# Two of the weights' four quarter sums made by accumulating DMAs, the other two written in place over them

## The chip, the cores and the metric

The kernel runs on one core of a Trainium2 chip. The metric is the device time of one execution in microseconds (us), and the median of three is compared. One core has a matrix engine (PE), a vector engine (DVE), a scalar engine (ACT), a general engine (POOL) and a sequencer that issues transfers (SP); each works through its own queue in order, and semaphores tie the queues together. Sixteen DMA engines move data between the memory and the on-chip buffers.

## The reference, cut to what matters

The reference is a decoder trunk of two layers over 528 tokens (16 learned ones and 512 given) of width 1024, all in float32:

```python
h = concat(meta_tokens, x)
for i in range(2):
    h = h + 0.5 * swiglu(rmsnorm(h, norm_ffn1[i]), ffn1_w_in[i], ffn1_w_out[i])   # 1024 -> 2 x 2816 -> 1024
    hn = rmsnorm(h, norm_mix[i])
    h = h + (retention(hn) if i == 0 else gla(hn))
    h = h + 0.5 * swiglu(rmsnorm(h, norm_ffn2[i]), ffn2_w_in[i], ffn2_w_out[i])
return rmsnorm(h, final_norm)[:, 16:]
```

`swiglu` is `(silu(x @ gate) * (x @ up)) @ out`. Retention and GLA are chunked linear attentions between projections of the same width. All that matters for the change is that nearly all the work is products of activations with large weights, each of which is read from memory once, and that every product is to be as exact as float32.

## The kernel before, in words

**Products.** The tokens lie along the free axis in two halves of 264 (256 in the last stage). A weight tile of 128x128 is the stationary operand of a matmul, the activations the moving one. For exactness each operand is held as two parts of a shorter format, `hi` and `lo`, and each product is three matmuls (`mm3`, lines 311 to 313): hi by hi, hi by lo, lo by hi.

**Units.** Most large products are done as a *unit* (`unit`, line 473 and on): two neighbouring weight tiles, cut in two halves each, make a 2x2 block of quarters a11, a12, a21, a22, the two token halves make the other side, and seven products replace eight (a Strassen-Winograd scheme). The seven use the pieces `a11, s1, s2, a12, s3, s4, a22`, where four are sums of the weights' quarters:

```python
SUMS = {"s1": ("a21", "a22"), "s2": ("s1", "a11"), "s3": ("a11", "a21"), "s4": ("a12", "s2")}
```

A piece is 128x512 (four 128x128 tiles), or 128x384 where the group of hidden tiles is six wide instead of eight. A unit has thus 7 x 4 x 3 = 84 matmuls, or 63 with narrow pieces. The program has 134 units, 24 of them narrow. The two SwiGLUs of each layer start with a phase of eight plain products (lines `p`, tiles `pf...`), during which the sums of the activations are prepared; then come units for gate (`Xf10g`, `QZf10g`), up (`...u`) and output (`...o`). Retention has some plain products and units, GLA plain products only.

**Weights.** The class `Weights` (line 54 and on) holds a plan of all pieces in the order of use. `_load` starts transfers of whole tiles of 128x1024 on SP's queue into four places (`raw`, 512 KB each, line 91); a unit needs two of them. `_piece` finds a quarter in a `raw` tile, or makes a sum with an addition on DVE into a `ws` tile (line 107). `_split` (lines 121 and 122) makes the two parts of a piece: `whi` is a copy with rounding on ACT, `wlo` the difference on DVE. There are seven places for `whi` and seven for `wlo`. After each product a call of `hook` asks for the split of the next four pieces, so the code runs at least that far ahead of the products; a place is free again when the last matmul on it has ended.

**Order.** Each engine's queue order is laid down when the program is built, by a scheduler that goes by the dependences, the program order and its own costs; code under `urgent()` is drawn forward by 300 steps. At run time every engine takes its queue strictly in order.

**Around the sums.** Besides the weights, DVE also adds up a unit's results (lines 664 to 676 for the output units), and in the last output group of a SwiGLU it prepares the next stage: for every finished row block of `x` it makes the `ula` part of the scaled activations (line 384) and a running sum of squares (line 392). Then come the statistics of the norm: matmuls `st_n` on PE, `ms_n` on DVE (line 427), a power on POOL (`rc`, line 429), `dg_n` on DVE (line 431), and `bc_n` on PE (line 438), which spreads the row factors. POOL has nothing else to do before the change.

Of the kernel before, what the change touches and what calls it, by code (L numbers as in the profile page):

```python
# [16 lines left out]
P = 128  # L17
# [37 lines left out]
class Weights:  # L55

    UNIT = ("a11", "s1", "s2", "a12", "s3", "s4", "a22")
    FIRST = ("s1", "s2", "a11", "a12", "s3", "s4", "a22")  # L60
    SUMS = {"s1": ("a21", "a22"), "s2": ("s1", "a11"), "s3": ("a11", "a21"), "s4": ("a12", "s2")}

    def __init__(self, tc, ctx, raw_bufs=4, bufs=7):
        self.nc = tc.nc
        self.raw_pool = ctx.enter_context(tc.tile_pool(name="wraw", bufs=raw_bufs))
        self.pool = ctx.enter_context(tc.tile_pool(name="wsplit", bufs=bufs))
        self.raw_bufs, self.bufs = raw_bufs, bufs
        self.chunks, self.raw = [], {}
        self.plan, self.parts, self.sums = [], {}, {}
        self.loaded = self.done = self.split = self.taken = 0  # L70
        self.live = set()
        self.sum_pool = None

    def add(self, key, ap):
        n = ap.shape[1]
        c = len(self.chunks)
        self.chunks.append(ap)
        for o in range(0, n, PW):
            self.plan.append((key, c, o, min(PW, n - o), o + PW >= n))

    def add_unit(self, key, ap1, ap2, order):
        c = len(self.chunks)
        self.chunks += [ap1, ap2]
        for q in order:
            self.plan.append((key + (q,), c, q, ap1.shape[1] // 2, {"s4": c, "a22": c + 1}.get(q)))

    def _load(self):
        while self.loaded < min(self.done + self.raw_bufs, len(self.chunks)):
            ap = self.chunks[self.loaded]
            t = self.raw_pool.tile([P, CW], F32, tag="raw", name=f"raw{self.loaded}")  # L90
            self.nc.sync.dma_start(t[:, :ap.shape[1]], ap)
            self.raw[self.loaded] = t
            self.loaded += 1

    def _piece(self, c, q):

        V = self.nc.vector
        if not isinstance(q, str):
            return self.raw[c][:, q:q + PW]
        n = self.chunks[c].shape[1] // 2  # L100
        if q[0] == "a":
            o = (int(q[2]) - 1) * n
            return self.raw[c + int(q[1]) - 1][:, o:o + n]
        if (c, q) not in self.sums:
            a, b = [self._piece(c, i) for i in self.SUMS[q]]
# [1481 lines left out]
```

## Time and profile before

| | us |
|---|---|
| median of three runs | 2142.69 (2142.47 to 2145.72) |
| the profiled execution | 2141.96 |
| its span in the trace | 2140.2 |
| PE busy in it | 2103.9 |
| DVE busy in it | 1868.0 |
| ACT busy in it | 1146.0 |
| POOL busy in it | 21.8 |
| bytes read from memory | 196.42 MB |

The page counts an engine as busy between the start and the modelled end of its instructions. Matmuls overlap, so PE counts as busy whenever one is in flight, and its idle time is only what remains. A row such as `PE Xf10o L311 <- ACT whi L121: 2.7, 3, 1.2` says: matmuls of line 311 into the tile `Xf10o` waited 2.7 us in all for ACT's `whi` of line 121, three times, 1.2 us at the longest. In a row of the table by stretches the number after x is how many instructions started in the stretch. Buffer numbers are left out of names, so `raw` stands for all raw tiles.

### The profile page before, as it was taken

The page shows a single profiled execution, that of the slowest core. Times are in us where ns is not written, and L with a number is a line of the kernel's source. Part 1 is how long each engine was busy: PE and PEld are TensorE (multiplying, and loading weights), DVE is VectorE, ACT ScalarE, POOL GpSimd, SP SyncE. Part 2 cuts the span into 40 slices and gives each one's busy share as a digit, 9 for nine tenths or more (in the row PEclk, how much of TensorE's full clock was granted, in tenths as well). Part 3 has the DMA queues.
Part 4 walks back from the last instruction along what each step waited for, and adds up shares of the span by engine and source line. Part 5 has one row for each costly group of instructions (what it writes and reads, how often), then busy time and mean ns, then how long its engine had stood idle before and what let it go on. Part 6 is the DMA issues. An engine that isn't in the chain of part 4 may idle for free.

```text
span 2140.2 us, 42535 instructions
## 1 busy us (share of the span) xinstructions
PE 2103.9 (98%) x16950; PEld 2069.3 (97%) x16950; DVE 1868.0 (87%) x3451; ACT 1146.0 (54%) x2220; POOL 21.8 (1%) x25
## 2 busy tenths in 40 slices
PE   8999999999999999999999999999999999999998
PEld 7999999999999999999998999999899999999998
DVE  7999999977686879999999999989876658999996
ACT  5656656443434354656566565656733235656654
POOL 0000000000000000000000000000000000000000
PEclk9999999999999999999999999999999999999999
DMA  4333323332222222232323233332312112233332
GB/s 142 98 110 100 103 93 92 100 110 82 97 80 96 83 71 79 90 109 99 109 93 96 80 109 103 97 107 86 122 60 66 63 62 78 87 121 99 104 109 75
DMA packets 59175, 201.26 MB, mean 94 GB/s; under 512 B 6624, under 2 KB 8032, under 8 KB 58976
## 3 DMA queue, kind: packets, MB, share of 16 engines
q1 hardware_dynamic: 57968, 195.26, 28.5%
q10 hardware_dynamic: 1008, 3.29, 0.5%
q8 instruction: 133, 2.18, 0.4%
q14 instruction: 66, 0.54, 0.1%
HBM read 196.42 MB, written 2.10 MB: 93 GB/s over the span
## 4 chain that ended last, share of the span: by engine, by line
PE 79%; DVE 15%; ACT 2%; DMA 2%; issue 2%; POOL 0%; SPq 0%; DVEq 0%; POOLq 0%; ACTq 0%
DVE wlo L122 4%; DVE ws L107 2%; PE po_r L313 1%; PE po_r L311 1%; PE po_r L312 1%; PE lv L1227 1%; DVE hf L340 1%; PE Xf21o L311 1%; PE Xf20o L311 1%; DMA raw<-in_f_in 1%; PE Xf20g L311 1%; PE Xf20g L312 1%; PE Xf20g L313 1%; PE Xf20u L311 1%; PE Xf11g L311 1%
## 5 line engine op out<-in xcount | busy, mean ns | idle before, releaser
L121 ACT CAST whi<-raw 128x512 fp32r<-128x512 f32 (+1 forms) x613 | 369.1, 608 | 393.2 <-PE gv L312 51.0
L121 ACT CAST whi<-ws 128x512 fp32r<-128x512 f32 (+1 forms) x536 | 322.3, 603 | 340.9 <-DVE ws L107 86.8
L122 DVE TENSOR_TENSOR wlo<-raw,whi 128x512 fp32r<-128x512 f32 (+1 forms) x613 | 402.9, 668 | 67.6 <-ACT whi L121 65.8
L122 DVE TENSOR_TENSOR wlo<-ws,whi 128x512 fp32r<-128x512 f32 (+1 forms) x536 | 349.5, 659 | 27.6 <-ACT whi L121 25.5
L107 DVE TENSOR_TENSOR ws<-raw 128x512 f32<-128x512 f32 (+1 forms) x134 | 88.6, 661 | 20.1 <-DMA raw<-in_f_in 13.6
L107 DVE TENSOR_TENSOR ws<-ws,raw 128x512 f32<-128x512 f32 (+1 forms) x134 | 88.6, 661 | 1.6
L107 DVE TENSOR_TENSOR ws<-raw,raw 128x512 f32<-128x512 f32 (+1 forms) x134 | 88.3, 659 | 0.4
L107 DVE TENSOR_TENSOR ws<-raw,ws 128x512 f32<-128x512 f32 (+1 forms) x134 | 88.2, 658 | 0.4
L313 PE MATMUL po_r<-ogh,wlo 128*128 128x264 f32 x256 | 72.9, 285 | 0.0
L311 PE MATMUL po_r<-ogh,whi 128*128 128x264 f32 x256 | 72.9, 285 | 0.0
L312 PE MATMUL po_r<-ogl,whi 128*128 128x264 f32 x256 | 72.6, 284 | 0.0
L339 ACT CAST hf<-yf 128x264 fp32r<-128x264 f32 (+2 forms) x86 | 45.0, 534 | 33.0 <-DVE yf L641 20.3
L311 PE MATMUL Xf10o<-hf,whi 128*128 128x264 f32 x176 | 51.1, 291 | 2.9 <-ACT whi L121 2.7
L311 PE MATMUL Xf11o<-hf,whi 128*128 128x264 f32 x176 | 51.1, 291 | 2.9 <-ACT whi L121 2.7
L311 PE MATMUL Xf20o<-hf,whi 128*128 128x264 f32 x176 | 51.1, 291 | 2.8 <-ACT whi L121 2.7
L313 PE MATMUL Xf20o<-hf,wlo 128*128 128x264 f32 x176 | 50.3, 286 | 0.0
L313 PE MATMUL Xf11o<-hf,wlo 128*128 128x264 f32 x176 | 50.3, 286 | 0.0
L313 PE MATMUL Xf10o<-hf,wlo 128*128 128x264 f32 x176 | 50.3, 286 | 0.0
L312 PE MATMUL Xf10o<-hf,whi 128*128 128x264 f32 x176 | 50.1, 285 | 0.0
L312 PE MATMUL Xf11o<-hf,whi 128*128 128x264 f32 x176 | 50.0, 285 | 0.0
L312 PE MATMUL Xf20o<-hf,whi 128*128 128x264 f32 x176 | 50.0, 285 | 0.0
L340 DVE TENSOR_TENSOR hf<-yf,hf 128x264 fp32r<-128x264 f32 (+2 forms) x86 | 49.3, 573 | 0.6 <-ACT hf L339 0.5
(732 smaller groups left out, 8671.6 us busy)
## 6 DMA issues: line engine op xcount, KB each, us to landing
raw<-in_f_in SPq DMA_DIRECT2D x176, 512.0 KB, 3.5
raw<-in_f_out SPq DMA_DIRECT2D x48, 512.0 KB, 3.6
raw<-in_ret_in SPq DMA_DIRECT2D x48, 512.0 KB, 3.4
raw<-in_f_out SPq DMA_DIRECT2D x48, 384.0 KB, 3.1
raw<-in_gla_in SPq DMA_DIRECT2D x25, 512.0 KB, 3.4
raw<-in_ret_o SPq DMA_DIRECT2D x16, 512.0 KB, 3.4
raw<-in_gla_o SPq DMA_DIRECT2D x8, 512.0 KB, 3.5
xa<-in_xT SPq DMA_DIRECT2D x8, 264.0 KB, 5.3
```

Of the source, the lines that this page charges most:

```text
L107: V.tensor_add(t, a, b)
L121: self.nc.scalar.copy(hi[:, :n], raw[:, :n])
L122: self.nc.vector.tensor_sub(lo[:, :n], raw[:, :n], hi[:, :n].bitcast(F32))
L311: nc.tensor.matmul(ps, lhsT=lh, rhs=rh, start=start, stop=False, **kw)
L312: nc.tensor.matmul(ps, lhsT=lh, rhs=rl, start=False, stop=False, **kw)
L313: nc.tensor.matmul(ps, lhsT=ll, rhs=rh, start=False, stop=stop, **kw)
L339: S.copy(hi, src)
L340: V.tensor_sub(lo, src, hi.bitcast(F32))
L1227: nc.tensor.matmul(ps[:, j, J * P:J * P + n], lhsT=Kt[:, j, J * P:(J + 1) * P], rhs=q, start=(J == 0), stop=(J == 3), skip_group_check=True)
```

## The change

In a unit, s1 and s3 are no longer made on DVE. For each unit there is a *pair*, a tile of 128x2x512 in one of three places. SP loads a11 into its first half and a22 into its second (two transfers of 256 KB). Then POOL issues one DMA that reads a21 from memory for both halves and adds it to what lies there. So the first half becomes s3 = a11 + a21 and the second s1 = a22 + a21, and ACT and DVE split them from there. The sums s2 and s4 remain additions on DVE, but written in place: s2 = s1 + a11 over s1 in the second half, and later s4 = s2 + a12 over s2.

For a11 and a12 the first tile is still loaded whole (`raw`), for a22 there is a new kind of place, `half`, of 128x512. The places are now 3 `raw`, 2 `half`, 3 `pair` and 6 instead of 7 for `whi` and `wlo`; the tiles for sums (four of them in a SwiGLU, three in retention) are gone. Each kind of place is refilled in its own order: `raw` and `pair` when the split of s4 has been asked for, `half` after that of a22. At the start of the program, the first three pairs and the first two halves are loaded ahead of the small constants `ident` and `causal` and of the fourth raw tile. `dynamic_dma_scratch_size` goes from 4096 to 2048.

```diff
     UNIT = ("a11", "s1", "s2", "a12", "s3", "s4", "a22")
     FIRST = ("s1", "s2", "a11", "a12", "s3", "s4", "a22")
-    SUMS = {"s1": ("a21", "a22"), "s2": ("s1", "a11"), "s3": ("a11", "a21"), "s4": ("a12", "s2")}
+    SUMS = {"s2": "a11", "s4": "a12"}
 
-    def __init__(self, tc, ctx, raw_bufs=4, bufs=7):
+    def __init__(self, tc, ctx, raw_bufs=3, half_bufs=2, pair_bufs=3, bufs=6):
...
     def add_unit(self, key, ap1, ap2, order):
-        c = len(self.chunks)
-        self.chunks += [ap1, ap2]
+        c = self.keys
+        self.keys += 1
+        n = self.width[c] = ap1.shape[1] // 2
+        self.loads["raw"].append((c, (ap1,)))
+        self.loads["pair"].append((c, (ap1[:, :n], ap2[:, n:], ap2[:, :n])))
+        self.loads["half"].append((c, (ap2[:, n:],)))
         for q in order:
-            self.plan.append((key + (q,), c, q, ap1.shape[1] // 2, {"s4": c, "a22": c + 1}.get(q)))
+            self.plan.append((key + (q,), c, q, n, {"s4": ["raw", "pair"], "a22": ["half"]}.get(q, [])))
 
     def _load(self):
...
+        nc = self.nc
+        for kind, loads in self.loads.items():
+            while self.begun[kind] < min(self.over[kind] + self.room[kind], len(loads)):
+                c, aps = loads[self.begun[kind]]
+                self.begun[kind] += 1
+                if kind == "pair":
+                    n = self.width[c]
+                    t = self.pair_pool.tile([P, 2, PW], F32, tag="pair", name=f"pair{c}")[:, :, :n]
+                    for i in range(2):
+                        nc.sync.dma_start(t[:, i], aps[i])
+                    nc.gpsimd.dma_start(t, aps[2].unsqueeze(1).broadcast_to([P, 2, n]), accum_op=ALU.add)
+                else:
+                    pool, w = (self.raw_pool, CW) if kind == "raw" else (self.half_pool, PW)
+                    t = pool.tile([P, w], F32, tag=kind, name=f"{kind}{c}")
+                    nc.sync.dma_start(t[:, :aps[0].shape[1]], aps[0])
+                self.tiles[kind, c] = t
 
     def _piece(self, c, q):
...
+        t = self.tiles["pair", c]
+        if q == "s3":
+            return t[:, 0]
+        if q in self.SUMS:
+
+            self.nc.vector.tensor_add(t[:, 1], t[:, 1], self._piece(c, self.SUMS[q]))
+        return t[:, 1]
...
-    nc = bacc.Bacc("TRN2", target_bir_lowering=False, num_devices=1, dynamic_dma_scratch_size=4096)
+    nc = bacc.Bacc("TRN2", target_bir_lowering=False, num_devices=1, dynamic_dma_scratch_size=2048)
```

The queues change with it. The line numbers shift by some 25: line 107 becomes 133, 121 and 122 become 146 and 147, 91 becomes 110 (pairs), 111 (accumulating DMA) and 115.

**DVE in the last output group of the first SwiGLU**, third of its four units. Before:

```order
L671 SCALAR_TENSOR_TENSOR xa<-suf10o_4671,xa 128x264
L392 TENSOR_TENSOR sqa_n_168<-sqa_n_168,sq_n_3_4790 128x528
L664 SCALAR_TENSOR_TENSOR xa<-suf10o_4671,xa 128x528
L107 TENSOR_TENSOR ws_64_4681<-raw_4463,raw_4479 128x384
L107 TENSOR_TENSOR ws_64_4697<-raw_4463,ws_64_4639 128x384
L107 TENSOR_TENSOR ws_66_4744<-raw_4597 128x384
L122 TENSOR_TENSOR wlo_4684<-ws_64_4681,whi_4683 128x384
L122 TENSOR_TENSOR wlo_4700<-ws_64_4697,whi_4699 128x384
L122 TENSOR_TENSOR wlo_4716<-raw_4479,whi_4715 128x384
L122 TENSOR_TENSOR wlo_4732<-raw_4581,whi_4731 128x384
```

The same place now:

```order
L695 SCALAR_TENSOR_TENSOR xa<-suf10o_4629,xa 128x264
L418 TENSOR_TENSOR sqa_n_188<-sqa_n_188,sq_n_3_4746 128x528
L688 SCALAR_TENSOR_TENSOR xa<-suf10o_4629,xa 128x528
L147 TENSOR_TENSOR wlo_4640<-pair_4284,whi_4639 128x384
L133 TENSOR_TENSOR pair_4284<-pair_4284,raw_4282 128x384
L696 SCALAR_TENSOR_TENSOR xa<-Xf10o_4627,xa 128x264
L147 TENSOR_TENSOR wlo_4655<-pair_4284,whi_4654 128x384
L147 TENSOR_TENSOR wlo_4675<-half_4442,whi_4674 128x384
L147 TENSOR_TENSOR wlo_4691<-raw_4422,whi_4690 128x384
L147 TENSOR_TENSOR wlo_4704<-pair_4424,whi_4703 128x384
```

Of three additions in a row (s3 and s4 of this unit, s1 of the next) one is left, s4; it stands behind the split of s3 instead of ahead of it.

**POOL**, at the norm ahead of retention. Before, the power is preceded by nothing but the power of the stage before:

```order
L429 TENSOR_TENSOR rc<-ms_n_311,half_neg 128x4
L429 TENSOR_TENSOR rc<-ms_n_315,half_neg 128x1
L429 TENSOR_TENSOR rc<-ms_n_4986,half_neg 128x4
L429 TENSOR_TENSOR rc<-ms_n_4990,half_neg 16x1
L356 TENSOR_TENSOR r_ro_6059<-ms_ro_6057,half_neg 88x6
```

Now:

```order
L111 DMA pair_4424<-in_f_out 128x2x384
L111 DMA pair_4540<-in_ret_in 128x2x512
L111 DMA pair_4660<-in_ret_in 128x2x512
L111 DMA pair_4782<-in_ret_in 128x2x512
L455 TENSOR_TENSOR rc<-ms_n_4939,half_neg 128x4
L455 TENSOR_TENSOR rc<-ms_n_4943,half_neg 16x1
L111 DMA pair_5627<-in_ret_in 128x2x512
```

The power now stands behind the accumulating DMAs of retention's first three units, and each of these waits for its pair's two loads.

**DVE at the start of the program**, at the first norm. Before:

```order
L427 TENSOR_SCALAR ms_n_311<-st_n_304 128x4
L427 TENSOR_SCALAR ms_n_315<-st_n_304 128x1
L431 TENSOR_TENSOR dg_n_310<-ident,rc 128x512
L431 TENSOR_TENSOR dg_n_310<-ident,rc 128x16
L122 TENSOR_TENSOR wlo_350<-raw_118,whi_349 128x512
```

Now:

```order
L453 TENSOR_SCALAR ms_n_328<-st_n_321 128x4
L453 TENSOR_SCALAR ms_n_332<-st_n_321 128x1
L147 TENSOR_TENSOR wlo_288<-raw_138,whi_287 128x512
L147 TENSOR_TENSOR wlo_292<-raw_138,whi_291 128x512
L147 TENSOR_TENSOR wlo_363<-raw_164,whi_362 128x512
L147 TENSOR_TENSOR wlo_367<-raw_164,whi_366 128x512
L457 TENSOR_TENSOR dg_n_327<-ident,rc 128x512
L457 TENSOR_TENSOR dg_n_327<-ident,rc 128x16
```

Four splits, of the fourth and fifth raw tile of the program, have come between `ms_n` and `dg_n`.

More of the change, by code (lines that the diff above doesn't have):

```diff
@@ L66, in __init__ @@
         self.pool = ctx.enter_context(tc.tile_pool(name="wsplit", bufs=bufs))
[L67 to L70, printed above, removed]
+        self.bufs = bufs
+        self.loads = {"raw": [], "half": [], "pair": []}
+        self.begun = dict.fromkeys(self.loads, 0)
+        self.over = dict.fromkeys(self.loads, 0)
+        self.room = {"raw": raw_bufs, "half": half_bufs, "pair": pair_bufs}
@@ L87, in _load @@
     def _load(self):
[L88 to L93, printed above, removed]
+        nc = self.nc
[14 more added lines that the diff above has]
+                self.tiles[kind, c] = t
@@ L95, in _piece @@
     def _piece(self, c, q):
-        V = self.nc.vector
         if not isinstance(q, str):
[L99 to L105, printed above, removed]
-            t = self.sum_pool.tile([P, PW], F32, tag="wsum", name=f"w{q}_{c}")[:, :n]
-            V.tensor_add(t, a, b)
-            self.sums[c, q] = t
@@ L109, in _piece @@
-        return self.sums[c, q]
+            return self.tiles["raw", c][:, q:q + PW]
+        n = self.width[c]
+        if q in ("a11", "a12"):
+            o = n if q == "a12" else 0
+            return self.tiles["raw", c][:, o:o + n]
+        if q == "a22":
+            return self.tiles["half", c][:, :n]
+        t = self.tiles["pair", c]
[3 more added lines that the diff above has]
+            self.nc.vector.tensor_add(t[:, 1], t[:, 1], self._piece(c, self.SUMS[q]))
@@ L115, in _split @@
             i = self.split
-            _, c, q, n, last = self.plan[i]
+            _, c, q, n, over = self.plan[i]
             self._load()
@@ L124, in _split @@
             self.split += 1
-            if last not in (None, False):
-                self.raw.pop(c if last is True else last)
-                self.done += 1
+            for kind in over:
+                del self.tiles[kind, c]
+                self.over[kind] += 1
                 self._load()
     def prime(self, n=None):
-        bufs = self.raw_bufs
-        self.raw_bufs = n or bufs
+        room = self.room
+        if n:
+            self.room = {"raw": n, "half": 0, "pair": 0}
         self._load()
-        self.raw_bufs = bufs
+        self.room = room
     def get(self, key):
@@ L847, in retention @@
     def retention(feed):
[L848 removed]
+        with tc.tile_pool(name="retp", bufs=1) as rp, psum_pool(4) as pp:
             other["pool"] = pp
[L850 removed]
             (a0, a1), (b0, b1) = HALVES
```

19 lines of the change are left out of this document (10 added, 9 removed).

## The prediction

> **What bounds the kernel now.** I read first the busy times and the chain, then what PE waits for, then the places where it waits, in time.
>
> ```profile
> span 2140.2 us, 42535 instructions
> PE 2103.9 (98%) x16950; PEld 2069.3 (97%) x16950; DVE 1868.0 (87%) x3451; ACT 1146.0 (54%) x2220; POOL 21.8 (1%) x25
> PE 79%; DVE 15%; ACT 2%; DMA 2%; issue 2%; POOL 0%; SPq 0%; DVEq 0%; POOLq 0%; ACTq 0%
> 963.00:1017.00 54.00, 54.00 (x447) 54.00 (x446) 53.55 (x97) 34.05 (x67) 0.00 (x0) 1.00 0.30 98
> ```
>
> PE is the bound: it is idle for 2140.2 - 2103.9 = 36.3 us. The fourth row, a stretch of 54 us in the middle of a SwiGLU, shows what that means for DVE: it is busy for 53.55 of 54 us and yet PE never stops; 447 matmuls in 54 us are one every 0.121 us. So taking work off DVE is worth nothing in such a stretch. It pays only where PE waits for a piece of weights:
>
> ```profile
> PE pf10g L311 <- ACT whi L121: 5.7, 1, 5.7
> PE pf10g L313 <- DVE wlo L122: 4.7, 2, 3.6
> PE Xf10o L311 <- ACT whi L121: 2.7, 3, 1.2
> PE Xf20o L311 <- ACT whi L121: 2.7, 3, 1.2
> PE Xf11o L311 <- ACT whi L121: 2.7, 3, 1.2
> PE bc_n L438 <- DVE dg_n L431: 0.5, 1, 0.5
> ```
>
> The 5.7 us are the first load of the program, which the change leaves. The 4.7 us lie in the first phase of plain products, which has no quarter sums. What is left is three times 2.7 us, once for each SwiGLU that prepares a next stage: 8.1 us. They lie in the last output group. For the first SwiGLU, the table by stretches, then DVE, ACT and PE around its longest stop:
>
> ```profile
> 333.00:372.50 39.50, 36.66 (x277) 34.34 (x276) 38.78 (x78) 25.77 (x56) 0.00 (x0) 1.00 0.26 81
> 333.00:372.50 39.50, 5.24 (x10) 1.00 0.26 81
> 357.80 0.70 DVE L664 SCALAR_TENSOR_TENSOR xa<-suf10o,xa 128x528 f32<-128x528 f32 x1
> 358.42 0.55 DVE L107 TENSOR_TENSOR ws<-raw,raw 128x384 f32<-128x384 f32 x1
> 358.88 0.55 DVE L107 TENSOR_TENSOR ws<-raw,ws 128x384 f32<-128x384 f32 x1
> 359.35 0.55 DVE L107 TENSOR_TENSOR ws<-raw 128x384 f32<-128x384 f32 x1
> 359.00 0.98 ACT L121 CAST whi<-ws 128x384 fp32r<-128x384 f32 x2 [1.32 <-DVE ws L107]
> 358.06 0.28 PE L313 MATMUL QZf10o<-hf,wlo 128*128 128x264 f32 x1
> 359.56 0.39 PE L311 MATMUL Xf10o<-hf,whi 128*128 128x264 f32 x1 [1.22 <-ACT whi L121]
> ACT whi L121 <- PE Xf10o L312: 17.9, 21, 1.4
> ```
>
> In these 39.5 us DVE is busy for 38.78 us, and 5.24 us of that are ten quarter sums (the second row is the same stretch with line 107 alone). At 358.42 DVE comes late to the sum for s3, ACT can only then begin its rounding, and PE stands from 358.06 to 359.56. The last row shows the other state: ACT waits for PE to give back a place for `whi`, so ahead of the overload all seven places are full.
>
> **The change part by part.** *Half of the sums leave DVE.*
>
> ```profile
> L107 DVE TENSOR_TENSOR ws<-raw x134: 542/683/695, 56.8 to 2083.0; 128x512 f32<-128x512 f32 x110, 128x384 f32<-128x384 f32 x24
> L107 DVE TENSOR_TENSOR ws<-raw,raw x134: 542/681/695, 66.3 to 2089.4; 128x512 f32<-128x512 f32 x110, 128x384 f32<-128x384 f32 x24
> ```
>
> These 268 additions go, at 0.68 us each (0.55 when narrow, see 358.42): 220 x 0.68 + 48 x 0.55 = 176 us of DVE's 1868 us. Nearly all of that was hidden behind PE, and is worth nothing. In an overloaded stretch five of ten sums go, 5 x 0.524 = 2.6 us, against a stop of 2.7 us.
>
> *Six places instead of seven* take one piece from the lead with which the stretch begins. A narrow piece is 9 matmuls, 9 x 0.121 = 1.09 us. If the lead was full this costs all of 1.09 us, if it was being rebuilt nothing: the gain is between 2.6 - 1.1 = 1.5 and 2.6 us for each of the three. I take 2.0 us, the middle, since the last row above shows the places full at some pieces and not at others: 3 x 2.0 = **6.0 us gained**. The bounds are 4.5 and, if all stops go, 8.1 us.
>
> *In place.* s2 is written over s1, so this addition now waits until ACT and DVE have split s1, and s4 over s2 likewise. DVE's queue has these splits ahead of the additions anyway, so while there is a lead it costs nothing; without one it costs at most one rounding on ACT (0.98 us for two, at 359.00), 0.5 us in a group that still stalls. I take 0 us.
>
> *The pair's way.* A new chain: SP loads a11 and a22, POOL issues, the accumulation lands. It starts when s4 of unit c is split, and unit c+3 wants its s1 17 pieces later: 17 x 12 x 0.121 = 24.7 us, for narrow pieces 18.5 us. The nearest rows:
>
> ```profile
> q1 hardware_dynamic: 57968, 195.26, 28.5%
> raw<-in_f_in SPq DMA_DIRECT2D x176, 512.0 KB, 3.5
> raw<-in_f_out SPq DMA_DIRECT2D x8, 256.0 KB, 2.7
> ident<-in_tri SPq DMA_DIRECT2D x1, 64.0 KB, 6.9
> ```
>
> The raw tile ahead takes 3.5 us, the two halves of the pair 2.7 us behind it, and the accumulation, which no row shows, between 3.5 us (a plain load of the same 512 KB) and 6.9 us (the slowest landing, a transfer queued behind others): 9.7 to 13.1 us, less than 18.5. I take 0 us for it; if the cover were gone, each unit would be late by what is missing.
>
> *The engines' time.* 195.26 MB took 28.5% of 16 engines, so all sixteen move 195.26 / (0.285 x 2140.2) = 0.32 MB/us. A wide unit now loads 1.31 MB plainly (before 1.05), 4.1 us of its 84 x 0.121 = 10.2 us. The accumulation writes 0.52 MB, 1.6 us as a plain copy. It is hidden below 10.2 - 4.1 = 6.1 us. The Trainium skill (Collectives: The Full Stack, section The bandwidth ceiling) says that a transfer with an addition has two source reads for one write and so runs at half the rate of a copy. No trace here shows that yet; by it the accumulation would take 3.2 us and the sum would be the same, with 2.9 us to spare instead of 4.5.
>
> *The start.* Before `ident` now come two halves and three pairs, 2.1 MB, less the fourth raw tile.
>
> ```profile
> 10.00:15.00 5.00, 4.59 (x26) 4.03 (x25) 5.00 (x9) 5.00 (x10) 0.00 (x0) 1.00 1.04 404
> 7.80 0.33 SPq L271 DMA_DIRECT2D ident<-in_tri  x1
> 23.14 0.78 DVE L431 TENSOR_TENSOR dg_n<-ident,rc 128x512 f32<-128x512 f32 x2 [1.06 <-POOL rc L429]
> 26.38 1.15 PE L438 MATMUL bc_n<-dg_n,ones 128*128 128x512 f32 x4
> ```
>
> There the engines move 404 GB/s, so 1.6 MB more cost 3.9 us: `ident` lands at about 7.8 + 6.9 + 3.9 = 18.6 us (issued at 7.80), ahead of `dg_n`. The fifth raw tile, behind which `dg_n` now stands, follows two raw tiles and two accumulations later, 2.1 to 3.1 MB, at 24 to 26 us, and two splits (0.68 us each, as the additions) and `dg_n` (0.78) take 2.1 us more: 26 to 28.4 us against `bc_n` at 26.38. That is 0 to 2.0 us of standing; I take 0.5 us, near the low end, because SP's loads are spread and the accumulations are shorter than a queue behind them.
>
> *POOL's power behind the DMAs.*
>
> ```profile
> L313 PE MATMUL Xf10o<-hf,wlo x176: 279/284/393, 119.7 to 372.7; 128*128 128x264 f32 x176
> 377.89 0.21 DVE L427 TENSOR_SCALAR ms_n<-st_n 128x4 f32<-128x4 f32 x2 [0.79 <-PE st_n L418]
> 378.20 1.90 POOL L429 TENSOR_TENSOR rc<-ms_n,half_neg 128x4 f32<-128x4 f32 x2 [354.56 <-DVE ms_n L427]
> 379.62 0.77 DVE L431 TENSOR_TENSOR dg_n<-ident,rc 128x512 f32<-128x512 f32 x2 [0.92 <-POOL rc L429]
> 380.36 1.45 PE L438 MATMUL bc_n<-dg_n,ones 128*128 128x512 f32 x4
> ```
>
> Here there is no slack: power, `dg_n` and `bc_n` follow each other, so a delay of POOL goes to PE. The DMAs ahead of it wait for loads that are released by s4 of the last unit, which with six places can be split up to six pieces, 6.5 us, ahead of its matmuls; the group's last matmuls start at 372.7 (first row), 5.5 us before the power. The loads need 3.5 + 2.7 us of these some 12. So they should have been issued. The cost lies between 0 and, if the last is just then waiting, 3.5 us, at three norms (378, 1174 and 1530 us). I take 0.3 us each, **0.9 us lost**.
>
> Sum: -6.0 + 0.5 + 0.9 = -4.6 us. The profiled execution took 2141.96 us, 1.8 us beyond its span and 0.7 us under the median of 2142.69; from the median that gives **2138 us**.
>
> **The rivals.** *A, nothing moves.* The smaller lead costs more than its middle, 1.1 us three times and the missing 0.5 us for writing in place, while POOL and the start cost 2 to 3 us: -4.5 + 1.5 + 2.5 = -0.5, so 2142 us. For it speaks the row at 963 us: work taken off DVE is not on the path. Against it, that the sums of 358.42 to 359.90 stand directly between PE and its weights.
>
> *B, POOL's queue as a new wait (slower).* If an accumulation's issue waits for its loads at the moment when a power is due, the norm is late by up to 3.5 us, at the four norms ahead of phases with units and at the four `bc_ro` of retention, and the start costs 2.0 us: with 2 us on the mean, 8 x 2 + 2.0 - 6.0 = +12 us, about 2155 us. It decides once a pair's two loads land later than `ms_n`; the queue order speaks for it, the estimated lead against it.
>
> *C, the DMA engines become the bound (slower).* Above 6.1 us for each accumulation (4.6 us when narrow) PE waits for pairs at every unit. At 8 us the loss is 110 x 1.9 + 24 x 1.5 = 245 us, 2385 us. For it speaks only that the trace has no accumulation; against it, that it would have to run at a quarter or less of a copy's rate.
>
> The Trainium skill (DMA: Bandwidth & Descriptors, section Issuing engines are not separate DMA queues) says that transfers of all issuing engines share the same sixteen engines. That is the mechanism of C; the row of 28.5% leaves room.
>
> **How the numbers follow.** Differences below 0.2%, 4.3 us, cannot be told from none here. My forecast has 0.58, of which 0.43 lies beyond 4.3 us of gain and 0.15 within; A has 0.17, all within; B 0.15 and C 0.10, both slower. So faster 0.43, same 0.32, slower 0.25. The forecast's own range is 2133 (all 8.1 us and a little more of the first phase) to 2142. The range for 8 in 10 goes down to 2131, where the 3.6 us of the first phase go too, and up to 2160, which takes in B and leaves out C.
>
> **What would show it.** In the profile after: DVE some 175 us less busy, near 1690, with line 107's successor (133) 268 times; PE's waits for `whi` in the three output groups down from 2.7 us to under 1; accumulating DMAs landing within 7 us; DMA share near 45 to 60%; `bc_n` and `bc_ro` waiting no longer than before. The forecast is wrong if rows appear in which ACT or DVE waits for DMA `pair` over whole stages (C), if POOL's `rc` starts later after `ms_n` than the 0.3 us of 377.89 to 378.20 (B), or if the three waits stay at 2.7 us (A).

## The result, and the profile after

The changed kernel takes **2154.38 us** (median of five runs, 2153.01 to 2158.36) against 2142.69 us of the kernel before (five runs, 2142.47 to 2145.72). The ratio is 1.0052, with a 95% interval of 1.0038 to 1.0067: 11.7 us slower, where 4.7 us faster was forecast. The time lies inside the range given, but the forecast had the wrong sign.

From the page and the table of transfers of the kernel after: span, busy times, the two large DMA queues, the additions left on DVE, and the landing of the accumulating transfers (KB each, median us from issue to landing).

```profile
span 2150.9 us, 43222 instructions
PE 2105.4 (98%) x16950; PEld 2070.5 (96%) x16950; DVE 1733.3 (81%) x3183; ACT 1134.1 (53%) x2220; POOL 184.6 (9%) x159
q1 hardware_dynamic: 96560, 228.83, 32.0%
q0 software_dynamic: 36448, 67.12, 19.6%
L133 DVE TENSOR_TENSOR pair<-pair,raw 128x512 f32<-128x512 f32 (+1 forms) x268 | 177.2, 661 | 2.4
pair<-in_f_in POOLq DMA_DIRECT2D x72, 512.0 KB, 6.5
pair<-in_f_out POOLq DMA_DIRECT2D x24, 512.0 KB, 7.6
```

The change did what it says: half the additions are gone, DVE is 134.7 us less busy, the accumulating transfers land in 6 to 8 us, and the engines that move data have room. PE is idle for 2150.9 - 2105.4 = 45.5 us, 9.2 us more than before. What PE waits for in the kernel after (us in all, times, longest):

```profile
PE Xf21o L337 <- ACT suf21o L527: 2.4, 3, 1.2
PE Xf10o L337 <- ACT whi L146: 1.6, 2, 1.4
PE pf11g L339 <- DVE wlo L147: 1.6, 1, 1.6
PE bc_n L464 <- DVE dg_n L457: 1.4, 3, 0.5
PE Xf10o L337 <- ACT suf10o L523: 1.3, 3, 0.8
PE pf21g L339 <- DVE wlo L147: 1.0, 1, 1.0
PE pf20g L339 <- DVE wlo L147: 0.9, 1, 0.9
PE QZf10o L338 <- DVE hf L366: 0.8, 1, 0.8
```

The three stops for `whi` did fall, from 2.7 to 1.6 us (`Xf20o` and `Xf11o` have the same row as `Xf10o`). But new rows have come: PE waits for `suf`, the copy by which ACT empties a PSUM bank, for `hf`, the hidden activations, and, more than before, for `wlo` in the phases of plain products (of the 1.6 us at `pf11g`, 1.1 us stood there before the change). None of the three is a sum or a transfer.

Where in the program it went shows when the start of the same matmul (the n-th on PE) is compared with the kernel before. The columns are stretches of the program; each number is what is lost (+) or gained (-) in it, in us, in the profiled execution of the kernel named. "Last" is the last output group of a SwiGLU with the norm behind it.

```
                              f1    last  reten-  f2    last   f1    last   GLA    f2    all
                              (0)   f1(0)  tion   (0)   f2(0)  (1)   f1(1)         (1)
after                        -3.0   +3.4   -0.3  +0.8   +4.6  -0.9   +2.0  -0.4   +4.0  +10.2
before with six places       +3.5   +2.7   -1.0  +2.1   +4.0  +1.4   +1.7  -1.5   +1.5  +14.5
before, sums in place        +5.8   +3.2   +0.1  +3.2   +2.2  +4.8   +4.6  -1.4   +9.4  +31.8
before without s1 and s3     +0.5    0.0   -0.5  -0.1   -2.3  -0.8   -1.5  -1.1   +1.1   -4.8
after, sums elsewhere        -1.9   +3.9   -0.1   0.0   +5.1  -2.1   +0.9  -0.4   +1.4   +6.8
... and seven places         -4.7   +1.3   +0.9  -1.1   -0.6  -2.1   +1.0  -1.4   -1.1   -7.8
```

The first row says: the first and third SwiGLU up to their last output groups gained (-3.0, -0.9), the last output groups, where the forecast had its 6 us of gain, lost 10.0 us, and the last SwiGLU, which prepares no next stage, lost 4.0. The other rows belong to the experiments.

A part of these numbers is PE's clock. In the kernel after, the granted clock is 0.5 for 3.4 us from 367.2 and again from 1165.9 us, in the last groups of the first two SwiGLUs, each time after one of the stops; in the kernel before it is full from 60.5 us almost to the end. The second of these stretches and the 3.4 us behind it (PE busy with its matmuls after x first, the granted clock third from the end of the row):

```profile
1165.90:1169.30 3.40, 3.40 (x17) 3.40 (x17) 2.61 (x6) 1.91 (x5) 0.00 (x0) 0.51 0.79 126
1169.30:1172.70 3.40, 3.40 (x30) 3.40 (x29) 3.10 (x7) 1.47 (x3) 0.00 (x0) 0.99 0.97 318
```

The 13 matmuls that are missing are worth 13 x 0.121 = 1.6 us, so some 3 of the 10.0 us lost in the last groups went this way, in time that counts as busy. e1_six and e2_in_place have three such stretches in last groups, "before without s1 and s3" and "after, sums elsewhere" have two, and "... and seven places" has none. At the start, the clock is at half from about 53.5 us on, for 6.8 us in the kernel before and for 3.4 us in the kernel after, which is already 1.3 us ahead at the first unit; so not all of the -3.0 is the units'. What sets such a stretch off isn't shown: e10_elsewhere_seven has a stop of 1.41 us as well, and no half clock behind it.

### The profile page after: what moved, and what is told of

It is laid out like the page before. It is cut to its first block, busy times and chain, and to the rows that moved or that the text cites. A ratio compares the mean times of both kernels' runs of the same rounds, so it can differ in the third digit from the quotient of the medians.

```text
span 2150.9 us, 43222 instructions
## 1 busy us (share of the span) xinstructions
PE 2105.4 (98%) x16950; PEld 2070.5 (96%) x16950; DVE 1733.3 (81%) x3183; ACT 1134.1 (53%) x2220; POOL 184.6 (9%) x159
## 3 DMA queue, kind: packets, MB, share of 16 engines
q1 hardware_dynamic: 96560, 228.83, 32.0%
q0 software_dynamic: 36448, 67.12, 19.6%
## 5 line engine op out<-in xcount | busy, mean ns | idle before, releaser
L146 ACT CAST whi<-pair 128x512 fp32r<-128x512 f32 (+1 forms) x536 | 322.4, 602 | 343.4 <-DVE pair L133 192.7
L147 DVE TENSOR_TENSOR wlo<-pair,whi 128x512 fp32r<-128x512 f32 (+1 forms) x536 | 355.5, 663 | 126.8 <-ACT whi L146 100.5
L146 ACT CAST whi<-raw 128x512 fp32r<-128x512 f32 (+1 forms) x479 | 290.2, 609 | 288.7 <-issue 39.5
L147 DVE TENSOR_TENSOR wlo<-raw,whi 128x512 fp32r<-128x512 f32 (+1 forms) x479 | 320.0, 672 | 85.9 <-ACT whi L146 81.7
L133 DVE TENSOR_TENSOR pair<-pair,raw 128x512 f32<-128x512 f32 (+1 forms) x268 | 177.2, 661 | 2.4
L111 POOL DMA_DIRECT2D pair<-in_f_in x72 | 87.5, 1216 | 767.5 <-DVE wlo L147 292.3
L111 POOL DMA_DIRECT2D pair<-in_f_out x48 | 58.1, 1211 | 462.4 <-DVE wlo L147 220.1
L147 DVE TENSOR_TENSOR wlo<-half,whi 128x512 fp32r<-128x512 f32 (+1 forms) x134 | 88.9, 663 | 8.2 <-ACT whi L146 5.6
L146 ACT CAST whi<-half 128x512 fp32r<-128x512 f32 (+1 forms) x134 | 80.6, 602 | 11.8 <-PE Xrv L338 4.0
L337 PE MATMUL Xf11o<-hf,whi 128*128 128x264 f32 x176 | 51.0, 290 | 3.3 <-ACT whi L146 1.6
```

The costliest lines, as they stand in the source:

```text
L111: nc.gpsimd.dma_start(t, aps[2].unsqueeze(1).broadcast_to([P, 2, n]), accum_op=ALU.add)
L133: self.nc.vector.tensor_add(t[:, 1], t[:, 1], self._piece(c, self.SUMS[q]))
L146: self.nc.scalar.copy(hi[:, :n], raw[:, :n])
L147: self.nc.vector.tensor_sub(lo[:, :n], raw[:, :n], hi[:, :n].bitcast(F32))
L337: nc.tensor.matmul(ps, lhsT=lh, rhs=rh, start=start, stop=False, **kw)
```

## The experiments

Theories: **S**, the sixth instead of the seventh place makes the loss; **I**, writing s2 and s4 in place makes it; **T**, the transfers of the pairs come late; and later **O**, the order of the queues sets what stands in the last groups, whatever DVE has to do. All times are medians, and "over before" is against the runs of the kernel before on the same chip.

| run | us | over before | ratio, 95% interval |
|---|---|---|---|
| the change | 2154.38 | +11.7 | 1.0052 (1.0038 to 1.0067) |
| e1_six | 2156.41 | +12.9 | 1.0066 (1.0053 to 1.0078) |
| e2_in_place | 2173.68 | +30.2 | 1.0143 (1.0129 to 1.0157) |
| e3_own_tiles | 2460.81 | +317.3 | 1.1489 (1.1463 to 1.1514) |
| e4_seven | 2223.71 | +80.2 | 1.0377 (1.0363 to 1.0391) |
| e5_six_in_place | 2182.20 | +40.2 | 1.0182 (1.0168 to 1.0196) |
| e6_elsewhere | 2149.25 | +7.2 | 1.0030 (1.0018 to 1.0041) |
| e7_seven_half | 2149.77 | +7.8 | 1.0034 (1.0022 to 1.0047) |
| e8_before_elsewhere | 2154.91 | +12.9 | 1.0058 (1.0044 to 1.0072) |
| e9_no_s1_s3 | 2135.28 | -6.8 | 0.9966 (0.9953 to 0.9978) |
| e10_elsewhere_seven | 2137.19 | -4.9 | 0.9975 (0.9966 to 0.9984) |
| e11_splits_forward | 2136.79 | -5.3 | 0.9972 (0.9961 to 0.9984) |
| e12_before_forward | 2177.48 | +35.4 | 1.0167 (1.0153 to 1.0181) |
| e13_seven_hi | 2143.34 | +0.9 | 1.0003 (0.9994 to 1.0012) |
| e14_seven_lo | 2148.40 | +6.0 | 1.0030 (1.0018 to 1.0041) |

### The kernel before with the small edits

e1_six is one number:

```diff
-    def __init__(self, tc, ctx, raw_bufs=4, bufs=7):
+    def __init__(self, tc, ctx, raw_bufs=4, bufs=6):
```

> The kernel before with six places for whi and wlo instead of seven, and nothing else: all four sums on DVE, in tiles of their own. Theory S (the shorter lead makes the loss): slower than before by 8 to 14 us, 2150 to 2157 us, with new waits of PE for whi and wlo in the last output groups. Theory I (writing in place makes the loss, since ACT and DVE then wait for each other at every sum): the lead costs only the 3 x 1.1 us that the prediction allowed for it, about 2146 us. Theory T (the transfers of the pairs come late): at most 2146 us as well, since no transfer is changed here.

Measured: +12.9 us, in the range of S. The waits of PE in e1_six from 1093 to 1215 us, the last output group of the second SwiGLU and what follows:

```profile
PE Xf20o L311 <- ACT whi L121: 2.6, 3, 2.0
PE pf11g L313 <- DVE wlo L122: 1.2, 1, 1.2
PE QZf20o L312 <- DVE hf L340: 1.0, 1, 1.0
PE Xf20o L311 <- ACT suf20o L497: 0.8, 1, 0.8
```

The rows for `suf` and `hf` are those that the change brought, here without any accumulating transfer. The timeline of e1_six at the start of that group, ACT and PE (start, length, idle time before and what ended it):

```profile
1140.80 0.51 ACT L121 CAST whi<-raw 128x384 fp32r<-128x384 f32 x1 [0.54 <-PE Xf20o L312]
1141.22 0.37 ACT L497 COPY suf20o<-Xf20o 128x264 f32<-128x264 f32 x1
1141.64 0.39 PE L311 MATMUL Xf20o<-hf,whi 128*128 128x264 f32 x1 [0.80 <-ACT suf20o L497]
1144.08 0.39 PE L312 MATMUL QZf20o<-hf,whi 128*128 128x264 f32 x1 [0.95 <-DVE hf L340]
1145.07 0.39 PE L311 MATMUL Xf20o<-hf,whi 128*128 128x264 f32 x1 [0.24 <-ACT whi L121]
```

And the same place in the kernel after, ACT and PE:

```profile
1134.48 0.51 ACT L146 CAST whi<-half 128x384 fp32r<-128x384 f32 x1 [0.57 <-PE Xf20o L338]
1134.89 0.37 ACT L523 COPY suf20o<-Xf20o 128x264 f32<-128x264 f32 x1
1135.32 0.39 PE L337 MATMUL Xf20o<-hf,whi 128*128 128x264 f32 x1 [0.80 <-ACT suf20o L523]
1137.74 0.39 PE L338 MATMUL QZf20o<-hf,whi 128*128 128x264 f32 x1 [0.93 <-DVE hf L366]
1138.73 0.39 PE L337 MATMUL Xf20o<-hf,whi 128*128 128x264 f32 x1 [0.24 <-ACT whi L146]
```

It is one pattern, to 0.03 us. ACT's next rounding has to wait until PE gives back a place (0.57 us); the copy that empties PE's bank stands behind that rounding in ACT's queue; PE then stands 0.80 us for the copy, 0.93 us for `hf` and 0.24 us for `whi`. So PE waits for an engine that waits for PE. With seven places PE had one short stop there: 0.53 us in the kernel before, 0.52 us in e10. These three stops are a part of the price only: in the table, e1_six loses 8.4 us in the last groups and 8.5 us in the rest of the SwiGLUs, where few waits are long enough to see.

e2_in_place writes s2 over s1 and s4 over s2, with everything else as before:

```diff
             a, b = [self._piece(c, i) for i in self.SUMS[q]]
-            t = self.sum_pool.tile([P, PW], F32, tag="wsum", name=f"w{q}_{c}")[:, :n]
+            t = {"s2": a, "s4": b}.get(q)
+            if t is None:
+                t = self.sum_pool.tile([P, PW], F32, tag="wsum", name=f"w{q}_{c}")[:, :n]
             V.tensor_add(t, a, b)
```

> The kernel before with seven places, four sums on DVE and no accumulating transfer; only s2 is written over s1 and s4 over s2, and the tile that they took stays free. Theory I: slower by 6 to 12 us, 2149 to 2155 us, with ACT's waits for the sum of line 107 well above the 86.8 us of before. Theory S and theory T: within 2 us of before, 2141 to 2145 us.

Measured: +30.2 us, two and a half times the most that theory I gave, and more than the whole change costs. ACT's waits for a sum, before and then in e2_in_place:

```profile
ACT whi L121 <- DVE ws L107: 86.8, 69, 3.4
```

```profile
ACT whi L123 <- DVE ws L109: 283.8, 191, 4.6
```

ACT rounds s1, DVE makes its `wlo`, only then may DVE add over it, and only then can ACT round s2; the two engines alternate at every unit. It costs PE in the middle of a SwiGLU too. The table by stretches for 100 to 330 us, before and then e2_in_place (PE is the first busy time, with its matmuls after x, DVE the third):

```profile
100.00:330.00 230.00, 229.90 (x1877) 228.56 (x1876) 219.64 (x392) 135.72 (x270) 0.00 (x0) 1.00 0.33 104
```

```profile
100.00:330.00 230.00, 225.36 (x1831) 223.18 (x1830) 215.49 (x382) 128.83 (x260) 0.00 (x0) 1.00 0.32 100
```

46 matmuls fewer, at 0.121 us each 5.6 us. e5_six_in_place has both edits of e1 and e2.

> The kernel before with both small edits and without the accumulating transfers: six places, s2 over s1 and s4 over s2, all four sums on DVE. Six places alone cost 13 us and writing in place alone 30 us. If the two prices add up: 2183 to 2189 us, and taking half of the sums off DVE is worth some 30 us against this kernel. If they are one price (a lost lead is lost once): 2168 to 2178 us, and the half of the sums is worth some 15 to 25 us. If taking sums off DVE is worth nothing, it would be at 2152 to 2158 us like the changed kernel.

Measured: +40.2 us against 12.9 + 30.2 = 43.1. The prices nearly add up where all sums are DVE's, and the accumulating transfers, with half of the sums off DVE, are worth 40.2 - 11.7 = 28.5 us against this kernel. The change's main idea pays here; its two small companions cost more than it brings.

e8_before_elsewhere puts s2 over a11 and s4 over s1. In this kernel s3 is still added on DVE, so what it adds to a21 is then s2 and no longer a11: the output is not the reference's, and s3 waits for s2 as well.

```diff
+            s1, a11 = self.sums.get((c, "s1")), self.raw[c][:, :n]
+            if q == "s2":
+                t = s1 if c in self.first else a11
+            elif q == "s4":
+                t = a11 if c in self.first else s1
+            else:
+                t = self.sum_pool.tile(...)
```

> The kernel before (seven places, all four sums on DVE) with s2 written over a11 in the raw tile and s4 over s1, where e2_in_place wrote s2 over s1 and s4 over s2. Theory I: no loss, 2140 to 2146 us, since the additions wait only for splits of two and four pieces ago. If any change of the tiles' places costs its 30 us through another order of the queues: 2160 to 2176 us.

Measured: +12.9 us, between the two expectations: it takes away more than half of e2's price. Because of that added wait of s3 it doesn't tell what is left.

### The changed kernel with the small edits taken back

e3_own_tiles and e4_seven had to make room by giving up the third pair.

```diff
-raw_bufs=3, half_bufs=2, pair_bufs=3, bufs=6):
+raw_bufs=3, half_bufs=2, pair_bufs=2, bufs=6):    # e3, with tiles of their own for s2 and s4
+raw_bufs=3, half_bufs=2, pair_bufs=2, bufs=7):    # e4
```

> The changed kernel, still with the accumulating transfers and six places, but s2 and s4 are written to two tiles of their own; to make room there are two pairs instead of three. Theory I: the loss goes, 2138 to 2144 us, and ACT's waits for the sums fall from 192.7 us to under 100. Theory S: stays at 2151 to 2157 us. Theory T: no better than 2154 us, and worse, since one pair less leaves the transfers less time.

> The changed kernel with seven places for whi and wlo instead of six; s2 and s4 still in place; two pairs instead of three, to make room. Theory S: the loss goes and what the prediction forecast shows, 2136 to 2143 us. Theory I: 2150 to 2155 us, since the order of ACT and DVE around the sums is unchanged. Theory T: 2154 us or more, with waits of ACT and DVE for the transfers into pair above those of the changed kernel (7.8 us of ACT).

Measured: +317 and +80 us. For S and I both are inconclusive, since the missing pair covers all else; what they tell is on T. DVE's waits in e3_own_tiles, and then the way of one pair in the kernel after, on SP's and POOL's queues:

```profile
DVE ws L138 <- DMA pair<-in_f_in: 136.2, 36, 7.4
DVE ws L138 <- DMA pair<-in_f_out: 98.6, 28, 6.6
```

```profile
1308.74 0.33 SPq L115 DMA_DIRECT2D raw<-in_f_in  x1
1310.16 1.25 SPq L110 DMA_DIRECT2D pair<-in_f_in  x2
1318.95 1.22 POOL L111 DMA_DIRECT2D pair<-in_f_in  x1 [9.93 <-DVE pair L133]
```

The accumulation issued at 1318.95 landed 9.6 us later, so this way took 19.8 us from the first load, one of the longest. From the issue and landing times in the trace, the way from the pair's first load to the landing of the accumulation took 13.1 us in the median of all 134 pairs (8.9 to 21.6), and the load of the raw tile that mostly goes ahead adds some 1.5 us. Three pairs cover 17 pieces, 24.7 us; two cover 10 pieces, 10 x 12 x 0.121 = 14.5 us, about the median way, so with two pairs many transfers come late. In e3_own_tiles it is DVE's addition that stands and waits for the pair (the two rows above), and PE's longest waits are then for `xa`, which DVE makes from PE's banks; in e4_seven it is ACT, for 53 us in 25 waits. That is a likely reason why e4_seven loses only a quarter as much, but no run separates it; the granted clock differs too, with a mean of 0.951 in e3_own_tiles and 0.985 in e4_seven. With three pairs the transfers are nearly always in time. In the kernel after, ACT's waits for them, and the longest step through a pair in the chain of waits (start, length), which lies in the last SwiGLU:

```profile
ACT whi L146 <- DMA pair<-in_f_in: 7.8, 10, 1.2
ACT whi L146 <- DMA pair<-in_f_out: 3.3, 4, 0.8
```

```profile
1889.62 9.74 DMA pair<-in_f_in
```

In the three last groups ACT waits for a pair only once, for 0.8 us, so T falls as the cause of the loss there; in the last SwiGLU's 4.0 us late pairs may have a part, but e10 below, with the same three pairs, gains 1.1 us there.

e6_elsewhere moves the two sums without needing room: a11 has been split two pieces before s2 is wanted, and s1 four before s4. Since s3 comes by transfer here, nothing else reads a11 any more.

```diff
-            self.nc.vector.tensor_add(t[:, 1], t[:, 1], self._piece(c, self.SUMS[q]))
+            a11 = self.tiles["raw", c][:, :n]
+            s2, s4 = (t[:, 1], a11) if c in self.first else (a11, t[:, 1])
+            if q == "s2":
+                self.nc.vector.tensor_add(s2, t[:, 1], a11)
+                return s2
+            self.nc.vector.tensor_add(s4, s2, self._piece(c, "a12"))
+            return s4
```

> The changed kernel, with only the places of the two sums moved, at no cost in memory: s2 is written over a11 in the raw tile (split two pieces earlier) and s4 over s1 in the pair (split four pieces earlier), so that neither addition waits for a split that has just been asked for. In the first unit of a SwiGLU, where a11 is split later, s2 stays over s1 and s4 goes over a11. Theory I (writing over the piece just split makes the loss): 2130 to 2144 us, ACT's waits for the sums of line 133's successor well under 192.7 us. Theory S (the shorter lead makes it): 2150 to 2157 us, as the changed kernel.

e7_seven_half has seven places and one half instead of two (`half_bufs=1, bufs=7`), with the sums in place.

> The changed kernel with seven places for whi and wlo, three pairs, and one half place instead of two to make room; s2 and s4 in place. Theory S: 2136 to 2144 us. Theory I: 2150 to 2158 us. If the single half place delays a22 (its load then has about 10 us), PE or ACT waits for half appear and the time is above 2160 us: then nothing follows on the places.

Measured: +7.2 and +7.8 us. Each takes away some 4 us of the change's 11.7, and neither theory has it alone. e10_elsewhere_seven has both.

> The changed kernel with both prices taken away at once: s2 over a11 and s4 over s1 (as in e6_elsewhere) and seven places (as in e7_seven_half, with one half place). e6 came out 5 us and e7 4.6 us faster than the changed kernel. If these add up: 2143 to 2146 us, no better than before. If the two small edits were all that stood in the way of the forecast: 2134 to 2139 us. Theory O: no faster than 2140 us.

Measured: -4.9 us, 2137.19 us, faster than both kernels. That is the forecast's 2138 us, but the number agrees by luck: the last row of the table shows the gain outside the last groups, where the forecast had none, and the last groups 1.7 us behind. The four runs make a square (those with seven places also have one half place instead of two):

| over before, us | seven places | six places |
|---|---|---|
| s2, s4 elsewhere | -4.9 (e10) | +7.2 (e6) |
| s2, s4 in place | +7.8 (e7) | +11.7 (the change) |

Either edit alone costs 12 to 13 us, the second on top of it 4 to 5. So the two prices don't add up; that both draw on one thing, the lead of ACT and DVE over PE, fits this but isn't shown. What "in place" does with seven places shows at s2 of the third of the four units in the second SwiGLU's last output group; first e7_seven_half, DVE, ACT and PE:

```profile
1150.73 0.55 DVE L147 TENSOR_TENSOR wlo<-pair,whi 128x384 fp32r<-128x384 f32 x1
1152.92 0.76 DVE L410 SCALAR_TENSOR_TENSOR ula<-xa,gains,uha 128x528 fp32r<-128x528 f32 x1
1154.56 0.55 DVE L133 TENSOR_TENSOR pair<-pair,raw 128x384 f32<-128x384 f32 x1
1155.15 0.51 ACT L146 CAST whi<-pair 128x384 fp32r<-128x384 f32 x1 [1.33 <-DVE pair L133]
1155.71 0.39 PE L337 MATMUL Xf20o<-hf,whi 128*128 128x264 f32 x1 [2.48 <-ACT whi L146]
```

and the same piece in e10_elsewhere_seven, DVE and PE:

```profile
1143.46 0.55 DVE L139 TENSOR_TENSOR raw<-pair,raw 128x384 f32<-128x384 f32 x1
1145.92 0.77 DVE L419 SCALAR_TENSOR_TENSOR ula<-xa,gains,uha 128x528 fp32r<-128x528 f32 x1
1147.14 0.39 PE L346 MATMUL Xf20o<-hf,whi 128*128 128x264 f32 x1
```

In e7 the addition can come only after the `wlo` of what it overwrites, and by then the next norm's `ula` and sums of squares stand in DVE's queue ahead of it; PE stops for 2.48 us. In e10 the addition stands ahead of `ula`, and PE hardly stops. At s2 of the next unit it is the other way round, 0.88 us in e7 and 1.41 us in e10; all stops for `whi` in the three last groups together come to 11.8 us in e7 and 5.7 us in e10. That is the smaller part of the price. Reckoned as in the table, e7 loses 7.3 us in the last SwiGLU, where e10 gains 1.1.

### The first term by itself, and the order

e9_no_s1_s3 is the kernel before without the additions of s1 and s3.

```diff
+            if q in ("s1", "s3"):
+                return self._piece(c, "a21")
```

> The kernel before with 268 additions left out and nothing else changed: the pieces s1 and s3 are just a21, so seven places, own tiles for s2 and s4, no accumulating transfer (the output is not the reference's). This is the prediction's first term alone. If that term holds, the stops of 2.7 us for whi in the last output groups go and it is 5 to 8 us faster, 2134 to 2138 us. Theory O (what stands there is set by the order of ACT's and DVE's queues, in which the norm's preparation comes ahead of sums and splits, and not by how much DVE has to do): 2140 to 2146 us, with stops of 2 us or more for whi left in the last output groups while DVE has gaps there.

Measured: -6.8 us, as the first term had it. In the table 3.8 of its 4.8 us lie in the last output groups and the norms behind them, where the term had them, and the rest of the SwiGLUs together gains nothing. But it isn't the stops: they stay, at 2.8 us in each of the three groups (`PE Xf10o ... <- ACT whi`), and with them theory O's half. The gain is there although the clock was at half for 3.4 us in two of the groups. What is seen to go are the 1.1 us for `wlo` at `pf11g` and as much for `whi` at `pg_gz`, the first products behind the second and third of the groups; the remainder is in waits too short to show as idle time.

```profile
PE Xf10o L313 <- ACT whi L123: 2.8, 2, 2.3
```

e11_splits_forward and e12_before_forward draw each sum and split forward, as the norm's preparation is.

```diff
+            with self.tc.high_priority(offset=HEAD_START):
                 raw = self._piece(c, q)
                 ...
```

> e10_elsewhere_seven with one more edit: each sum with its split (addition, whi, wlo) is drawn forward by the same 300 steps as the norm's preparation, so that it no longer stands behind that in the queues of ACT and DVE. Theory O: the stops for whi in the last output groups go, 5 to 8 us under e10, 2131 to 2139 us. If it is the amount of work or the transfers: as e10. Against it: evacuations of PSUM that then stand behind splits would make PE wait for suf, at up to 1.2 us a unit, and the time would be above e10.

> The kernel before with only that edit: each sum with its split drawn forward by 300 steps. Theory O: what the forecast wanted from taking sums off DVE is had by order alone: 2133 to 2138 us, with the three stops of 2.7 us under 1 us each. If the stops come from DVE being overloaded: 2141 to 2146 us, the stops only move to other tiles.

Measured: e11 -5.3 us, no different from e10's -4.9; e12 +35.4 us. O holds for the stops and falls for the time. In e11 the stops for `whi` fall to 0.5 us in each of the three groups, from 1.9 us in e10, and by the reckoning of the table these groups gain 4.6 us where e10's lose 1.7; but new waits come elsewhere, 2.8 us for `ula` in the first unit and 2.1 us in retention among them, and the time stays. With all sums on DVE the order does harm.

### Which engine's place

e13_seven_hi and e14_seven_lo are e6_elsewhere with a seventh place for `whi` alone and for `wlo` alone.

```diff
-            hi = self.pool.tile([P, PW], F32R, tag="hi", name=f"whi{i}")
-            lo = self.pool.tile([P, PW], F32R, tag="lo", name=f"wlo{i}")
+            hi = self.pool.tile([P, PW], F32R, tag="hi", name=f"whi{i}", bufs=7)
+            lo = self.pool.tile([P, PW], F32R, tag="lo", name=f"wlo{i}", bufs=6)
```

> e6_elsewhere with a seventh place for whi alone (wlo keeps six; both half places stay). It tells by which engine the sixth place costs its 12 us (e6_elsewhere 2149.25 us, e10_elsewhere_seven 2137.19 us). If ACT's queue is what stops (a rounding waits for PE to free a place for whi, and the evacuation of PSUM behind it is late): most of the 12 us comes back, 2137 to 2142 us, and PE's waits for suf at the start of the last output groups go. If DVE's queue does (a difference waits for a place for wlo): 2146 to 2150 us. If both are needed: between, 2142 to 2148 us.

> The other half: e6_elsewhere with a seventh place for wlo alone. If ACT's queue is what stops: 2146 to 2150 us, as e6_elsewhere. If DVE's does: 2137 to 2142 us. If both: as e13_seven_hi, between 2142 and 2148 us.

Measured: +0.9 and +6.0 us, against +7.2 of e6 and -4.9 of e10. ACT's place gives back 6.3 us, DVE's 1.2 us, both together 12.1 us: half goes with ACT's place alone, hardly anything with DVE's alone, and the rest needs both, or comes from what else sets e10 apart: one half place instead of two, and a code that may ask for seven pieces ahead where e13 and e14 stop at six.

## Why the prediction was wrong, step by step

**What bounds the kernel now: right on DVE, too coarse on PE.** PE was the bound, but its busy share doesn't say that nothing is left to gain in such a stretch. The table by stretches for 1220 to 1440 us, in the kernel before, after, in e10_elsewhere_seven, and in e9_no_s1_s3:

```profile
1220.00:1440.00 220.00, 219.78 (x1788) 218.11 (x1787) 208.64 (x370) 130.00 (x256) 0.00 (x0) 1.00 0.33 102
```

```profile
1220.00:1440.00 220.00, 219.90 (x1796) 218.99 (x1795) 186.99 (x328) 129.89 (x259) 24.66 (x21) 1.00 0.68 174
```

```profile
1220.00:1440.00 220.00, 220.00 (x1808) 220.00 (x1807) 192.79 (x328) 129.17 (x255) 25.40 (x21) 1.00 0.69 178
```

```profile
1220.00:1440.00 220.00, 218.91 (x1794) 218.46 (x1794) 186.53 (x327) 131.00 (x256) 0.00 (x0) 1.00 0.32 104
```

PE is busy for 219.78 of 220 us before, and yet 20 matmuls, 2.4 us, behind e10. A matmul takes 0.28 us and the next starts 0.12 us after it, so a wait of up to some 0.16 us leaves no idle time. The stretch of 54 us that the prediction showed was one without such waits; the count of matmuls over a long stretch would have shown them. So the 8.1 us of stops were not all there was to gain: e10's 7.8 us in the table of stretches come mainly from the SwiGLUs outside their last groups (-4.7, of which 1.6 lie ahead of the first unit, -1.1, -2.1, -1.1 us), while the last groups together lose 1.7 us. But it isn't the work taken off DVE that brings them: e9, with the same additions gone, has 6 matmuls more than before in this stretch, and from 100 to 330 us one fewer. "Worth nothing in such a stretch" stands, then; what else in e10 gains there, no run shows.

**Half of the sums leave DVE (6.0 us gained): size and place about right, the way there wrong.** e9 gains 6.8 us, most of it in and behind the last groups, but with the stops of 2.7 us still there. In the kernel after these stops did shrink to 1.6 us each; that gain was covered by what came new in the same groups. DVE fell by 134.7 us and not by 176: the prediction multiplied durations, where an addition starts 0.46 us after the one ahead (its own rows 358.42, 358.88, 359.35) and overlaps it. The wide ones start 0.60 us apart, which makes 220 x 0.60 + 48 x 0.46 = 154 us; the other 20 us aren't broken down.

**Six places instead of seven (0 to 1.09 us in each of three groups, 0.6 us taken): the step that failed.** It measured 12.1 us (e10 to e6, with the second half place) and 12.9 us (e1, with nothing else changed), where 1.8 us were taken and 3.3 us were the bound. The bound counted one piece of lead, 9 matmuls, once in a group. What happens is that ACT and PE come to wait for each other, with the emptying of PSUM and `hf` behind the rounding; that adds three stops at the start of a last group, 2.0 us in all where 0.5 us stood before, and stops for `wlo` in the phases of plain products (1.6, 0.9 and 1.0 us, against 1.1 us at the first of these before). Behind the stops come the stretches at half clock, 1.6 us each, for which the prediction had no term. The rest of the price lies outside the last groups, in waits that don't show. The row `ACT whi L121 <- PE Xf10o L312: 17.9, 21, 1.4` was read as "all seven places are full, so there is lead to spare"; it also says that ACT's queue stands still for PE, with whatever lies behind it.

**In place (0 us): the other step that failed.** It measured 12.7 us with seven places (e10 to e7) and 4.5 us with six (e6 to the change). "DVE's queue has these splits ahead of the additions anyway" is true, but the addition then waits for ACT's rounding and DVE's difference of the piece just asked for, and ACT for the addition. ACT waits 192.7 us for sums in the kernel after, 99.2 us in e10. That it already waited 86.8 us for them, in 69 waits, stood in the profile before and wasn't used.

**The pair's way (0 us): right for nearly the whole program, by less than was thought.** From the raw tile's load to the landing it takes 14.7 us in the median instead of the 9.7 to 13.1 estimated, and the longest come near the 24.7 us of cover. POOL issues the accumulation 6.0 us (median) after the pair's first load, where 2.7 us were reckoned for the two loads, and it lands 6.3 us after that.

**The engines' time (0 us): right.** The accumulations moved 67.12 MB in 19.6% of 2150.9 us, 0.16 MB/us; the plain loads 228.83 MB in 32.0%, 0.33 MB/us. A wide unit's accumulation thus takes 0.52 / 0.16 = 3.3 us of the sixteen engines, under the 6.1 us that were free. The rule cited from the Trainium skill (Collectives: The Full Stack, section The bandwidth ceiling), half the rate of a copy, which that section states for the reducing step of a collective, agrees with these two rows.

**The start (0.5 us lost): somewhat high**, at the first `bc_n` the kernel after is 0.2 us behind the kernel before. **POOL's power (0.9 us lost): not seen.** In the kernel after, the norm that stands behind the accumulating transfers:

```profile
379.44 0.22 DVE L453 TENSOR_SCALAR ms_n<-st_n 128x4 f32<-128x4 f32 x2 [0.74 <-PE st_n L444]
379.75 1.93 POOL L455 TENSOR_TENSOR rc<-ms_n,half_neg 128x4 f32<-128x4 f32 x2 [3.59 <-DVE ms_n L453]
```

The power starts 0.31 us after `ms_n`, as before, and at the other norms 0.25 to 0.32 us after it. `bc_n` waits 1.4 us in all instead of 0.5, but it waits 1.4 us in e2_in_place too, which has no such transfer.

**The rivals.** B and C did not happen. That the measured time is B's 2155 us is chance: B's sign, a power later than 0.3 us after `ms_n`, is not there. A's numbers for the lead and for writing in place, 3.3 and 1.5 us, were too small by the same misreadings. That these two edits could turn the sign was not among the rivals.

**The sum, as measured:** the sums off DVE -6.8 us (e9), pairs, start and POOL with one half place +1.9 us (e9 to e10, 1.4 taken), six places, with the second half place, and writing in place +16.6 us (e10 to the change, 1.8 taken): +11.7 us. The +1.9 us is the difference of two medians whose intervals overlap, and can't be told from none.

How much of the two prices comes from the waits themselves and how much from the order that the scheduler builds under them can't be told apart: every run that changed a dependence or a number of places also changed the order, and no run held it fixed.

## What to carry to other kernels

Room that is paid for out of buffers between engines can cost more than what it buys: price a lost place by what stands behind the waiting instruction in the in-order queue, and whether the engine waited for waits back. A number that comes out right in one variant (e10) proves no mechanism: look where in the program the time was gained. Write a result over a buffer whose readers ended several steps ago, not over the one being read; with that and the seventh place kept (e10), the change is 4.9 us faster than before. To see whether a busy engine is at its peak, count its instructions over a long stretch instead of reading its busy share.

## What the runs showed of the hardware that was not expected

PE's granted clock fell to half for 3.4 us after some of its stops, although none of these in the last groups of the kernel after is longer than 1.41 us; a matmul then starts 0.22 us after the one ahead instead of 0.12.

An accumulating DMA of 512 KB lands 6.1 to 7.6 us after its issue, against 3.4 to 4.5 us for a plain load of that size, and uses the sixteen engines for twice a copy's time (0.16 against 0.33 MB/us). With it the engines' busy share in the units rose from 0.33 to 0.68, and yet DVE's differences kept their length: 683 ns before, 687 ns after.

```profile
L122 DVE TENSOR_TENSOR wlo<-ws,whi 128x512 fp32r<-128x512 f32 x440 | 297.5, 683 | 27.0 <-ACT whi L121 25.0
```

```profile
L147 DVE TENSOR_TENSOR wlo<-pair,whi 128x512 fp32r<-128x512 f32 x440 | 302.4, 687 | 111.4 <-ACT whi L146 85.6 <-PE Xf10u L338 6.1 <-PE Xf20u L338 6.1
```
